# SyncE's queue in program order through the attention stage, pages fetched group by group, and gathers placed earlier in the program

## The chip, the cores and the metric

The kernel runs on one core of one Trainium2 chip. The metric is the device time of one execution in microseconds; of several executions the median is taken. Engines are named as in the profile: PE (matrix engine), DVE, ACT and POOL (vector, scalar and GpSimd engine), and SP, whose queue starts almost all transfers between HBM and on-chip memory. POOL starts the remaining ones, the gathers by a table of indices.

## What is computed

One layer of a decoder, for a prompt of 512 tokens and, with the same weights, for 8 samples that each have one new token and 1024 cached ones. D_MODEL is 1024, every tensor is f32. Two attention mixers read the same modulated input; "a" has three branches (compressed, selected, window), "b" (MoBA) picks blocks:

```python
h = x * (1.0 + scale[:, None, :]) + shift[:, None, :]
parts = jnp.split(h @ w_in, np.cumsum(IN_WIDTHS)[:-1], axis=-1)
(a_q, a_kc, a_vc, a_ks, a_vs, a_kw, a_vw, a_g, a_z, b_q, b_k, b_v, b_z, m_a, m_b) = parts
...
y_a = (o_a.reshape(bsz, t, NSA_WIDTH) * jax.nn.silu(a_z)) @ w_up_a
y_b = (o_b.reshape(bsz, t, MOBA_WIDTH) * jax.nn.silu(b_z)) @ w_up_b
mixed = (jax.nn.sigmoid(m_a) * y_a + jax.nn.sigmoid(m_b) * y_b) @ w_out
x_new = layer_norm(DEEPNORM_ALPHA * x + gate[:, None, :] * mixed, ln_g, ln_b)
```

For the samples the past rows of the caches come page by page: `rows = pool[page_table, layer]`. The layer also returns the new K and V rows.

## The kernel before

The whole layer is one program. Its parts, in the order of time:

- **Up to about 160 us**: the modulation, the compression network (`phi_*`) of the prompt and of the samples' cached rows (the stage `phis`), and the first projections.
- **About 160 to 520 us, the attention stage**: a loop over eight steps `pi`. Each runs `attend(pi)` (the prompt's attention of one or two heads at a time), a share of `dec()` (the samples' attention over their cached rows) and the projections listed in `FILLS[pi + 1]`. `merge` interleaves these three generators by the costs that their `yield`s name, so the numbers `ATT`, `DEC_SHARE` and `DEC` and the `yield`s decide in which order the program is written.
- **About 520 to 555 us**: `FILLS[9]`, that is the last projections (`bz2`, `bz3`, `m7`) and the gates `g0` to `g3`, merged with the rest of `dec()`.
- **To the end**: the matrices `w_up`, `w_out`, the normalisation and the output.

A **projection** (`dense`) is 48 matmuls of 260 columns into `d`: the 128 weight columns of one `w_cols` item, split into a high and a low half (`hl`; ACT makes the high part on L302, DVE or POOL the low part on L219), against the transposed input `hTh`, `hTl`. The items are loaded by the object `W`, a `Feed` over a ring of four buffers `raw`. `g0` to `g3` are items of `ada_g`, used unsplit by the matmuls `s<-raw,cs`. What a projection leaves goes on by name: `m0` to `m6` go through ACT as `mg` (L666) to HBM (`m_d`, L669) and are read back (`m_d` to `kd`, `v2`, `m`, L1376) when the attention's buffers are free; K and V rows are copied out as `ok<-ev` (L575); V rows are turned on PE and copied by DVE (`v`, L600, and `vnew`, L605). Work of that kind that need not follow at once is put on a list by `post`, and popped during the next projection.

The **samples' part** `dec()` reads 64 KB to 1 MB pieces of the caches into two buffers `raw` of 2048 columns, by the object `C`, also a `Feed`: `take` loads the next item when one is taken. The items, in order: four of `slck` (16 pages each), two of `wink`, 16 of `mobk` (4 pages each), then `slcv` gathers and `winv`, then 16 of `mobv` (4 pages each). Each item feeds one group of matmuls `e<-raw,...` on PE. `load_pages` reads a page's number from the page table into a register of SP (L728) and starts one transfer per page (L732). A `slcv` item is two gathers by POOL of 512 KB each (L1160). They stand behind the last POOL instruction `p` of the attention that was written so far (`issue_after(D["pool"].ins)`). `dec()` ends with `dec_b`: own scores and values of the new tokens (`snew`, `np`), then the `mobv` groups.

The **order of the queues**: a scheduler at build time orders the instructions of each engine by its own estimate of their times, except where the program fixes an order. Before, the program fixes PE's order through the attention stage (`behind`, L181 to L194) and leaves SP's order to the scheduler, with `tc.high_priority()` on the loads of `W` (`W.first`), on `ok<-ev` and on the writes to `m_d`. When the attention ends, `behind` is switched off; PE's further work is only kept behind the last attention instruction (`D["floor"]`). On POOL, `qx` (L996) makes the second operand for the scores of the next heads, and `p` (L1045) scales the probabilities of each score tile. `prepare(pi + 1)` issues `q`, `qx` and the `band` table (L983, L450) for the next step.

Of the kernel before, what the change touches and what calls it, by code (L numbers as in the profile page):

```python
# [46 lines left out]
DEC_SHARE = [0.155, 0.28, 0.405, 0.53, 0.59, 0.645, 0.74, 0.855]  # L47
DEC, DEC_PACE = 57600.0, 0.85
# [115 lines left out]
def build(tc, A):  # L164
# [3 lines left out]
    glue, behind = [False, None], [False, None]  # L168
# [12 lines left out]
    def in_turn(i):  # L181

        D["pe"] = i
        if "floor" in D:
            order(i, D["floor"])
# [38 lines left out]
    with ExitStack() as es:  # L224
# [35 lines left out]
        class Feed:  # L260


            def __init__(self, items, pool, tag, width, nraw, nhl=0):
                self.pool, self.tag, self.width, self.nraw, self.nhl = pool, tag, width, nraw, nhl
                self.loads = [(fn, n) for fn, n, _ in items]
                self.units = [(i, v) for i, (_, _, vs) in enumerate(items) for v in vs]
                self.raw, self.part = {}, {}
                self.nl = self.ns = 0
                self.used = -1
                self.apart = ()  # L270
                self.after = None
                self.first = False

            def load_to(self, i):
                while self.nl <= i and self.nl < len(self.loads):
                    fn, n = self.loads[self.nl]
                    t = self.pool.tile([128, self.width], F32, name="raw", tag=self.tag + "r", bufs=self.nraw)
                    if self.first:
                        with tc.high_priority():
                            fn(t[:, :n])  # L280
                    elif self.after is None:
# [41 lines left out]
        def w_item(n):  # L323
            if n == "ag":
                return (lambda t: nc.sync.dma_start(t, A["w_ag"])), 192, [lambda r: r[:, :192]]
# [8 lines left out]
            return (lambda t: nc.sync.dma_start(t, src)), 1024, HALVES  # L334
# [255 lines left out]
        def gen_v(name, vi):  # L590
            ev = evac((yield from dense(name)), name)

            def prompt():
# [6 lines left out]
                nc.vector.tensor_copy(v, p)  # L600

            def rest():
                p = p_d()
                tr(p[:NS, :128], ev[:, T:], ident)
                nc.vector.tensor_copy(vnew[:, vi, :], p[:NS, :128])  # L605
# [52 lines left out]
        def gen_m(c):  # L658
# [3 lines left out]
            for i, n in enumerate(("ma", "mb")):  # L662
# [4 lines left out]
                if "fm" not in D:  # L667
                    with tc.high_priority():
                        nc.sync.dma_start(m_d[c][:, i], to)  # L669
# [53 lines left out]
        def load_pages(outs, name, k0, step=1):  # L723
# [7 lines left out]
            for out, page in zip(outs, pages):  # L731
                dyn.append(nc.sync.dma_start(out, A[name][bass.ds(page, 1)].rearrange("a p c -> p (a c)")))  # L732
# [16 lines left out]
        def units(n, rhs):  # L749

            us = []
            for kv in range(2):
                u = p_s()
                for l in range(8):
                    for j, (wa, x) in enumerate(((w1h, 0), (w1l, 0), (w1h, 1))):
                        r = rhs(kv, x, l)
                        o = u[:, :n + 2] if n == 64 else u[:, :n]
                        mm(o, wa[:, kv, l, :], r, l == 0 and j == 0, l == 7 and j == 2)
# [29 lines left out]
        def phi_prompt(kc, vc):  # L788
            ut = []
            for kv, ev in enumerate((kc, vc)):  # L790
# [8 lines left out]
                for x, cp in enumerate((nc.scalar.copy, nc.vector.tensor_copy)):  # L799
                    v = f32(eh[:, x]).rearrange("p (u l s) -> p l u s", l=8, s=2)  # L800
                    for g in range(2):
                        for l2 in range(2):
                            cp(ut[kv][OWN[l2], x, :, g * 32:g * 32 + 32], v[OWN[g], :, :, l2])
            gl = yield from units(64, lambda kv, x, l: ut[kv][:, x, l, :])
# [167 lines left out]

        W.first = True
# [5 lines left out]
        def prepare(pi):  # L979
# [3 lines left out]
            nc.sync.dma_start(bt, A["band"][pi])  # L983
# [49 lines left out]
        def probs(j, i, n, s):  # L1033
# [11 lines left out]
            D["pool"] = nc.gpsimd.tensor_scalar(pr, pr, sm[:, 3:4], j.gate(i), op0=OP.mult, op1=OP.mult)  # L1045
# [64 lines left out]
        def step(j, extra=()):  # L1110
# [12 lines left out]
            for f, arg in extra:  # L1123
                slots[2].append(lambda f=f, arg=arg: f(arg))
# [6 lines left out]
        def attend(pi):  # L1131
            js = jobs_of(pi)
            if pi < 7:
                prepare(pi + 1)
            for k, j in enumerate(js):
                ex = []
                if pi < 4 and k == 0:
                    ex = [(cmp_score, pi)]
                if pi < 4 and k == 1:
                    ex = [(cmp_turn, pi)]  # L1140
# [6 lines left out]
        def page_item(name, firsts, width, step=1):  # L1147
            def fn(t):
                for i, k in enumerate(firsts):
                    load_pages([t[:, c * width:c * width + width] for c in range(4 * i, 4 * i + 4)], name, k, step)  # L1150
            return fn, 2048, [None]

        def plain_item(name, k):
            return (lambda t: nc.sync.dma_start(t, A[name][k])), 2048, [None]

        def slcv_item(i):
            def fn(t):
                with tc.issue_after(D["pool"].ins):
                  for k in range(2):
                    nc.gpsimd.indirect_dma_start(out=t[:, k * 1024:k * 1024 + 1024], out_offset=None, in_=A["slcv"],  # L1160
                                                 in_offset=bass.IndirectOffsetOnAxis(ap=vidx[:, 2 * i + k:2 * i + k + 1], axis=0))
            return fn, 2048, [None]

        C = Feed([page_item("slck", [(4 * q + b4) * 8 + hf * 4 for b4 in range(4)], 128)
                  for hf in range(2) for q in range(2)]
                 + [plain_item("wink", q) for q in range(2)]
                 + [page_item("mobk", [b * 8 + hf * 4], 512) for hf in range(2) for b in range(NS)]
                 + [i for q in range(2) for i in (slcv_item(2 * q), slcv_item(2 * q + 1), plain_item("winv", q))]
                 + [page_item("mobv", [4 * q * 8 + k], 512, 8) for q in range(2) for k in range(8)],
                 de, "c", 2048, CRAW)  # L1170
        C.apart = set(range(len(C.loads)))

# [15 lines left out]
        def new_p(d):  # L1188
# [5 lines left out]
            yield 300  # L1194
# [7 lines left out]
        def dec_a():  # L1202

            C.load_to(1)
            yield 2500
            xs = de.tile([128, 1026], F32, name="xs", tag="x")
            for hf in range(2):
                s = p_e()
                for q in range(2):
# [9 lines left out]
            nc.sync.dma_start(xw[:, :512], A["bw"])  # L1219
            less_last(xw[:, :512], xw[:, :512], brow[:, 0:1])  # L1220
            for q in range(2):
# [4 lines left out]
                if q == 0:  # L1226
                    yield 1000
# [3 lines left out]
            nc.vector.tensor_copy(xs[:, 1024:1025], snew[:, 0:1])  # L1231
# [8 lines left out]
            for g in range(2):  # L1240
                nc.vector.tensor_copy(view(zm[OWN[g]], g, [[NS * 32, 4], [34, NS]]), y[OWN[g], 4:8, T:])
# [6 lines left out]
            for hf in range(2):  # L1248
                s = p_e()
                for b in range(NS):  # L1250
# [6 lines left out]
                    yield 1000  # L1257
# [7 lines left out]
            for q in range(2):  # L1265
# [7 lines left out]
                yield 2700  # L1273
# [7 lines left out]
                yield 1400  # L1281

        def dec_b():
# [3 lines left out]
            nc.sync.dma_start(masks, A["cst"][:, NC2:NC3])  # L1287
# [7 lines left out]
            yield 300  # L1295
            total()
            yield 300
# [26 lines left out]
            for q in range(2):  # L1324
                o = p_e()
                for k in range(8):
# [4 lines left out]
                    yield 1000  # L1331
# [25 lines left out]
        for pi in range(8):  # L1357
# [7 lines left out]
            done = DEC_SHARE[pi]  # L1365
        at_es.close()
        behind[0] = False
        D["floor"] = D["pe"]
# [385 lines left out]
```

## Time and profile before

| | |
|---|---|
| median of 3 runs | 690.44 us (687.56 to 694.62) |
| the profiled execution, its own time | 692.0 us |
| its span in the trace | 690.2 us |
| mean clock granted to PE | 0.953 of full speed |
| DVE, ACT, POOL busy | 320.3, 297.0, 287.4 us |
| moved by DMA | 124.80 MB, 181 GB/s over the span |

A table of waits names, per engine and line, what an instruction stood waiting for. A table of windows gives for each stretch of time the busy time of each engine, the clock that PE was granted, and how busy the DMA engines were (1.00 is all 16 of them all the time). A line of the timeline starts with the start and the length of a piece of work in microseconds, then engine, line, operation and the tensors (out<-in); brackets at its end give the engine's idle time before it and what ended it. PE's matmuls overlap, so the length of one is longer than its share of a run of them. "SPq" and "POOLq" mean the issuing queue, and `x10` that ten like pieces stand in one line.

### The profile page before, as it was taken

The page shows a single profiled execution, that of the slowest core. Times are in us where ns is not written, and L with a number is a line of the kernel's source. Part 1 is how long each engine was busy: PE and PEld are TensorE (multiplying, and loading weights), DVE is VectorE, ACT ScalarE, POOL GpSimd, SP SyncE. Part 2 cuts the span into 40 slices and gives each one's busy share as a digit, 9 for nine tenths or more (in the row PEclk, how much of TensorE's full clock was granted, in tenths as well). Part 3 has the DMA queues.
Part 4 walks back from the last instruction along what each step waited for, and adds up shares of the span by engine and source line. Part 5 has one row for each costly group of instructions (what it writes and reads, how often), then busy time and mean ns, then how long its engine had stood idle before and what let it go on. Part 6 is the DMA issues. An engine that isn't in the chain of part 4 may idle for free.

```text
span 690.2 us, 13240 instructions
## 1 busy us (share of the span) xinstructions
PE 613.8 (89%) x4709; PEld 514.0 (74%) x4709; DVE 320.3 (46%) x817; ACT 297.0 (43%) x678; POOL 287.4 (42%) x327
## 2 busy tenths in 40 slices
PE   5999799999766999999993939989998879999993
PEld 3788799999754788777763838986775568899673
DVE  3464455525732744544641414665430115655167
ACT  3365455534442654544550525554441124333422
POOL 2033747523532434334542624534420126566546
PEclk9999999999997999999996979999999799999997
DMA  8984566413555627767743445423978873244303
GB/s 316 398 290 140 142 179 196 126 62 105 183 164 165 231 95 239 238 206 249 227 136 115 142 137 204 148 99 96 313 255 295 312 290 120 73 156 152 113 1 124
DMA packets 63956, 124.80 MB, mean 181 GB/s; under 512 B 8402, under 2 KB 26642, under 8 KB 63378
## 3 DMA queue, kind: packets, MB, share of 16 engines
q1 hardware_dynamic: 62482, 119.76, 52.5%
q0 software_dynamic: 1408, 4.20, 2.0%
q8 instruction: 37, 0.61, 0.4%
q14 instruction: 29, 0.24, 0.1%
HBM read 114.34 MB, written 9.58 MB: 180 GB/s over the span
## 4 chain that ended last, share of the span: by engine, by line
PE 69%; DMA 9%; DVE 6%; issue 5%; SPq 4%; POOL 4%; ACT 3%; POOLq 0%; DVEq 0%; ACTq 0%
PE d L172 39%; PE s L172 11%; PE e L172 6%; PE pt L193 3%; SPq L732 3%; PE o L172 3%; PE o L175 3%; DMA raw<-slcv,vidx 2%; DMA raw<-mobv 2%; PE pt L172 2%; PE e L175 1%; DMA u<-ada_ss 1%; POOL hl L219 1%; DMA m_d<-mg 1%; DMA craw<-cmp 1%
## 5 line engine op out<-in xcount | busy, mean ns | idle before, releaser
L172 PE MATMUL d<-hTh,hl 128*128 128x260 f32 (+1 forms) x1408 | 282.0, 296 | 4.6 <-ACT hl L302 2.8
L172 PEld LDWEIGHTS d<-hTh,hl 128*128 128x128 f32 (+1 forms) x1408 | 223.3, 192 | 33.4 <-issue 22.8
L172 PE MATMUL d<-hTl,hl 128*128 128x260 f32 (+1 forms) x704 | 202.2, 288 | 0.0
L172 PEld LDWEIGHTS d<-hTl,hl 128*128 128x128 f32 (+1 forms) x704 | 134.8, 191 | 1.1 <-issue 0.8
L219 POOL TENSOR_TENSOR hl<-raw,hl 128x512 fp32r<-128x512 f32 x54 | 70.9, 1313 | 74.2 <-ACT hl L302 60.7
L302 ACT CAST hl<-raw 128x512 fp32r<-128x512 f32 (+1 forms) x111 | 68.0, 617 | 77.7 <-PE d L172 57.9
L1043 ACT ACTIVATE p<-s,sm 128x512 f32<-128x512 f32 (+1 forms) x96 | 50.7, 529 | 93.9 <-DVE sm L1040 88.1
L1045 POOL TENSOR_SCALAR p<-p,sm,gp 128x512 f32<-128x512 f32 (+1 forms) x64 | 41.1, 642 | 108.0 <-DVE sm L1044 105.8
L219 DVE TENSOR_TENSOR hl<-raw,hl 128x512 fp32r<-128x512 f32 (+1 forms) x57 | 53.3, 936 | 48.3 <-ACT hl L302 47.3
L172 PE MATMUL d<-yh,hl 128*128 128x260 f32 x256 | 46.8, 284 | 1.8 <-DVE ev L1421 1.8
L1040 DVE CUSTOM_DVE_ANT_0 s<-s,band 128x256 f32<-128x256 f32 (+1 forms) x48 | 17.5, 364 | 64.8 <-PE s L172 62.8
L172 PE MATMUL e<-raw,tp 128*32 128x512 f32 (+1 forms) x40 | 20.5, 598 | 25.6 <-DMA raw<-slcv,vidx 21.3
L172 PEld LDWEIGHTS d<-yh,hl 128*128 128x128 f32 x256 | 39.6, 188 | 3.3 <-DVE ev L1421 2.2
L1038 DVE TENSOR_REDUCE sm<-s 128x1 f32<-128x256 f32 (+1 forms) x48 | 17.0, 355 | 52.4 <-PE s L172 50.9
L193 PE MATMUL pt<-cst,p 128*128 128x128 f32 x240 | 39.7, 281 | 0.7 <-DVE pp L1054 0.7
L1045 POOL TENSOR_SCALAR p<-p,sm,cst 128x512 f32<-128x512 f32 (+3 forms) x32 | 20.5, 641 | 41.6 <-DVE sm L1044 34.9
L172 PE MATMUL d<-yl,hl 128*128 128x260 f32 x128 | 35.9, 284 | 0.0
L172 PE MATMUL s<-u,w1h 128*128 128x256 f32 (+1 forms) x160 | 30.7, 287 | 4.3 <-ACT u L839 2.7
L219 POOL TENSOR_TENSOR u<-craw,u 128x512 fp32r<-128x512 f32 x16 | 22.1, 1389 | 29.5 <-ACT u L839 29.5
L193 PEld LDWEIGHTS pt<-cst,p 128*128 128x128 f32 x240 | 29.0, 144 | 6.5 <-DVE sm L1044 2.5
L172 PE MATMUL s<-kd,q 128*128 128x512 f32 (+1 forms) x96 | 32.8, 342 | 0.0
L1054 ACT COPY pp<-pt 128x512 f32<-128x512 f32 (+1 forms) x48 | 23.0, 480 | 19.9 <-PE pt L193 19.7
(414 smaller groups left out, 1168.0 us busy)
## 6 DMA issues: line engine op xcount, KB each, us to landing
raw<-w_cols SPq DMA_DIRECT2D x46, 512.0 KB, 3.9
raw<-mobk SPq DMA_DIRECT2D x64, 256.0 KB, 4.1
raw<-mobv SPq DMA_DIRECT2D x64, 256.0 KB, 4.2
craw<-cmp SPq DMA_DIRECT2D x64, 128.0 KB, 2.3
u<-ada_ss SPq DMA_DIRECT2D x12, 512.0 KB, 9.0
raw<-slck SPq DMA_DIRECT2D x64, 64.0 KB, 2.1
raw<-ada_g SPq DMA_DIRECT2D x8, 512.0 KB, 5.1
raw<-w_up SPq DMA_DIRECT2D x8, 512.0 KB, 5.2
```

Of the source, the lines that this page charges most:

```text
L172: i = mmraw(out, lhsT, rhs, start=start, stop=stop, skip_group_check=True)
L175: i = mmraw(out, lhsT, rhs, start=start, stop=stop, skip_group_check=True)
L193: return in_turn(nc.tensor.transpose(out, x, unit))
L219: (nc.gpsimd if eng == "p" else nc.vector).tensor_sub(out, x, f32(hi))
L302: nc.scalar.copy(h, src)
L732: dyn.append(nc.sync.dma_start(out, A[name][bass.ds(page, 1)].rearrange("a p c -> p (a c)")))
L1038: nc.vector.tensor_reduce(sm[:, 0:1], s[:, :b], axis=AX, op=OP.min)
L1040: nc.vector.tensor_tensor_reduce(out=s[:, b:n], in0=s[:, b:n], in1=j.band[:, 256 - (n - b):], scale=1.0, scalar=top, op0=OP.add, op1=OP.mi ...
L1043: nc.scalar.activation(pr, s[:, :n], AF.Exp, scale=-1.0, bias=sm[:, 1:2], accum_out=sm[:, 2:3])
L1045: D["pool"] = nc.gpsimd.tensor_scalar(pr, pr, sm[:, 3:4], j.gate(i), op0=OP.mult, op1=OP.mult)
L1054: j.copied[gi] = (nc.scalar.copy if COPY_ENG[gi] == "a" else nc.vector.tensor_copy)(t[:, :n], p[:, :n])
```

## The change

- **SP's queue.** A new helper `ld` starts every transfer of SP; between the opening of the attention's pools and the end of `FILLS[9]` each is chained behind the one before it in the program (`queue`). The high priorities of the loads go. `ok<-ev` and the writes to `m_d` are put on the `post` list, so they stand in the program during the next projection.
- **Pages.** `Feed` for the caches is replaced by `Pages`: the next item is fetched behind the group that frees its buffer, page quad by page quad, with a `yield` after each quad.
- **Gathers.** They stand behind the last but one `p` instead of the last, and by `Pages` they come behind the group that frees their buffer.
- **PE's order** stays fixed until the end of `FILLS[9]`; the `floor` goes. The posts are emptied at the attention's end, and the reads of `m_d` stand there in SP's order.
- **Smaller moves.** `prepare(pi + 1)` goes from ahead of a step to the end of its first job; copies of V rows get a high priority on DVE; the `zm` copies come later; the first matmul of a compression unit is ordered; shares and `yield`s change.

```diff
-DEC_SHARE = [0.155, 0.28, 0.405, 0.53, 0.59, 0.645, 0.74, 0.855]
-DEC, DEC_PACE = 57600.0, 0.85
+DEC_SHARE = [0.1, 0.236, 0.375, 0.51, 0.575, 0.63, 0.765, 0.89]
+DEC, DEC_PACE = 58800.0, 0.9
...
+    def ld(out, x):
+
+        i = nc.sync.dma_start(out, x)
+        if queue[0]:
+            if queue[1] is not None:
+                order(i, queue[1])
+            queue[1] = i
+        return i
...
-            with tc.high_priority() if W.first else ExitStack():
-                nc.sync.dma_start(A["ok"][KOUT.index(name)], ev)
+            post(lambda: ld(A["ok"][KOUT.index(name)], ev))
...
-                nc.vector.tensor_copy(v, p)
+                with tc.high_priority() if behind[0] else ExitStack():
+                    nc.vector.tensor_copy(v, p)
...
-                    with tc.high_priority():
-                        nc.sync.dma_start(m_d[c][:, i], to)
+                    post(lambda to=to, i=i: ld(m_d[c][:, i], to))
...
-            if pi < 7:
-                prepare(pi + 1)
             for k, j in enumerate(js):
-                ex = []
+                ex = [(3, prepare, pi + 1)] if pi < 7 and k == 0 else []
...
-                with tc.issue_after(D["pool"].ins):
...
+                with tc.issue_after(D["pool"][-2].ins):
...
+        class Pages:
+            def __init__(self, items):
+                self.items, self.tiles = iter(items), []
+            def fetch(self, cost=0):
+                item = next(self.items, ())
+                if item:
+                    t = de.tile([128, 2048], F32, name="raw", tag="cr", bufs=CRAW)
+                for fn in item:
+                    fn(t)
+                    yield cost / len(item)
+                if item:
+                    self.tiles.append(t)
+                else:
+                    yield cost
+            def take(self):
+                return self.tiles.pop(0)
...
-            C.load_to(1)
-            yield 2500
+            drain(C.fetch())
+            yield from C.fetch(2600)
...
-                    yield 1500
+                    yield from C.fetch(1200 if hf and q else 2000)
...
-                    yield 1000
+                    yield from C.fetch(1600 if hf and b == NS - 1 else 850)
...
-                yield 2700
+                yield from C.fetch()
+                yield from C.fetch(2300)
...
-                    yield 1000
+                    yield from C.fetch(1000)
...
+        while posts:
+            posts.pop(0)()
         at_es.close()
-        behind[0] = False
-        D["floor"] = D["pe"]
...
-            nc.sync.dma_start(TM[c], m_d[c])
+            ld(TM[c], m_d[c])
         merge(Flow(fills(FILLS[9]), fill_cost(FILLS[9])), Flow(part(2.0), max(1.0, (1 - done) * DEC / DEC_PACE)))
-        D.pop("floor")
-        assert not posts
+        while posts:
+            posts.pop(0)()
+        behind[0] = queue[0] = False
```

Two places show how instructions move. The first is POOL's queue around the first two pairs of `slcv` gathers (`raw<-slcv`, two of 512 KB in each row). In the kernel before, the second pair, `raw_4851`, stands behind `qx_4405` and the `p` that follows it:

```order
L1160 DMA raw_4755<-slcv,vidx_77 128x1024 x2
L1045 TENSOR_SCALAR p_4769<-p_4769,sm_4766,gp_80 128x384
L1045 TENSOR_SCALAR p_4791<-p_4791,sm_4789,gp_80 128x256
L996 TENSOR_TENSOR qx_4405<-y_95,q2_4404 64x512
L1045 TENSOR_SCALAR p_4830<-p_4830,sm_4828,gp_80 128x128
L1160 DMA raw_4851<-slcv,vidx_77 128x1024 x2
L1045 TENSOR_SCALAR p_4894<-p_4894,sm_4891,gp_80 128x512
```

In the changed kernel the same stretch of POOL's queue reads:

```order
L1163 DMA raw_4749<-slcv,vidx_77 128x1024 x2
L1051 TENSOR_SCALAR p_4732<-p_4732,sm_4729,gp_80 128x512
L1051 TENSOR_SCALAR p_4764<-p_4764,sm_4761,gp_80 128x384
L1163 DMA raw_4801<-slcv,vidx_77 128x1024 x2
L1051 TENSOR_SCALAR p_4786<-p_4786,sm_4784,gp_80 128x256
L1002 TENSOR_TENSOR qx_4561<-y_95,q2_4560 64x512
L1051 TENSOR_SCALAR p_4832<-p_4832,sm_4830,gp_80 128x128
```

The second pair has moved from behind `qx` to ahead of it, three instructions earlier, and the first pair stands one `p` earlier.

The second place is SP's queue at the attention's end, where the last write to `m_d`, its seven reads, the gates' `ada_g` and the weights of `bz3` (`raw<-w_cols`) stand among the `mobv` pages. In the kernel before, with the pages and register loads between them left out, the queue reads:

```order
L1376 DMA v2_6608<-m_d_94 128x1040
L334 DMA raw_6475<-ada_g 128x1024
...
L334 DMA raw_6738<-ada_g 128x1024
L1376 DMA v2_6610<-m_d_94 128x1040
L669 DMA m_d_94<-mg_6592 128x520
...
L1376 DMA m_6612<-m_d_94 128x1040
L1376 DMA m_6614<-m_d_94 128x1040
...
L334 DMA raw_6740<-w_cols 128x1024
L334 DMA raw_6746<-ada_g 128x1024
```

In the changed kernel, from the last write to `m_d` on, again without the pages (two `mobv` items stand between `raw_6671` and `raw_6768`):

```order
L199 DMA m_d_94<-mg_6645 128x520
L199 DMA kd_6655<-m_d_94 128x1040
L199 DMA kd_6657<-m_d_94 128x1040
L199 DMA kd_6659<-m_d_94 128x1040
L199 DMA v2_6661<-m_d_94 128x1040
L199 DMA v2_6663<-m_d_94 128x1040
L199 DMA m_6665<-m_d_94 128x1040
L199 DMA m_6667<-m_d_94 128x1040
L199 DMA raw_6671<-ada_g 128x1024
...
L199 DMA raw_6768<-ada_g 128x1024
L199 DMA raw_6770<-ada_g 128x1024
L199 DMA raw_6772<-w_cols 128x1024
```

All seven reads now stand together behind the last write, and three of the first four `ada_g` loads behind the reads; before, four `ada_g` loads and five reads stood ahead of that write.

More of the change, by code (lines that the diff above doesn't have):

```diff
@@ L166, in build @@
     mmraw = nc.tensor.matmul
-    glue, behind = [False, None], [False, None]
+    glue, behind, queue = [False, None], [False, None], [False, None]
     def mm(out, lhsT, rhs, start, stop):
@@ L604, in rest @@
                 tr(p[:NS, :128], ev[:, T:], ident)
-                nc.vector.tensor_copy(vnew[:, vi, :], p[:NS, :128])
+                with tc.high_priority() if behind[0] else ExitStack():
+                    nc.vector.tensor_copy(vnew[:, vi, :], p[:NS, :128])
             post(prompt)
@@ L731, in load_pages @@
             for out, page in zip(outs, pages):
-                dyn.append(nc.sync.dma_start(out, A[name][bass.ds(page, 1)].rearrange("a p c -> p (a c)")))
+                dyn.append(ld(out, A[name][bass.ds(page, 1)].rearrange("a p c -> p (a c)")))
         def phi_start():
@@ L757, in units @@
                         o = u[:, :n + 2] if n == 64 else u[:, :n]
-                        mm(o, wa[:, kv, l, :], r, l == 0 and j == 0, l == 7 and j == 2)
+                        before = D["pe"]
+                        i = mm(o, wa[:, kv, l, :], r, l == 0 and j == 0, l == 7 and j == 2)
+                        if kv == l == j == 0:
+                            order(i, before)
                     yield 333
@@ L971, in build @@
         at = D["at"] = open_pool(at_es, "at", "right")
-        W.first = True
+        queue[0] = True
         pc = at.tile([128, T], F32, name="pc")
@@ L1147, in page_item @@
         def page_item(name, firsts, width, step=1):
[L1148 to L1151, printed above, removed]
+            return [lambda t, i=i, k=k: load_pages([t[:, c * width:c * width + width] for c in range(4 * i, 4 * i + 4)], name, k, step)
+                    for i, k in enumerate(firsts)]
         def plain_item(name, k):
-            return (lambda t: nc.sync.dma_start(t, A[name][k])), 2048, [None]
+            return [lambda t: ld(t, A[name][k])]
@@ L1156, in slcv_item @@
         def slcv_item(i):
             def fn(t):
-                with tc.issue_after(D["pool"].ins):
[L1159 to L1170, printed above, removed]
@@ L1171, in build @@
-        C.apart = set(range(len(C.loads)))
+                with tc.issue_after(D["pool"][-2].ins):
+                    for k in range(2):
+                        nc.gpsimd.indirect_dma_start(out=t[:, k * 1024:k * 1024 + 1024], out_offset=None, in_=A["slcv"],
+                                                     in_offset=bass.IndirectOffsetOnAxis(ap=vidx[:, 2 * i + k:2 * i + k + 1], axis=0))
+            return [fn]
+        class Pages:
[14 more added lines that the diff above has]
+                return self.tiles.pop(0)
@@ new lines, in build @@
+        C = Pages([page_item("slck", [(4 * q + b4) * 8 + hf * 4 for b4 in range(4)], 128)
+                   for hf in range(2) for q in range(2)]
+                  + [plain_item("wink", q) for q in range(2)]
+                  + [page_item("mobk", [b * 8 + hf * 4], 512) for hf in range(2) for b in range(NS)]
+                  + [i for q in range(2) for i in (slcv_item(2 * q), slcv_item(2 * q + 1), plain_item("winv", q))]
+                  + [page_item("mobv", [4 * q * 8 + k], 512, 8) for q in range(2) for k in range(8)])
@@ L1230, in dec_a @@
             nc.vector.tensor_add(xs[:, 896:1024], xs[:, 896:1024], bdn[:, 0:128])
-            nc.vector.tensor_copy(xs[:, 1024:1025], snew[:, 0:1])
+            late = nc.vector.tensor_copy(xs[:, 1024:1025], snew[:, 0:1])
             xv = xs[:, 64:960].rearrange("p (j c) -> p j c", j=14)
@@ L1240, in dec_a @@
             for g in range(2):
-                nc.vector.tensor_copy(view(zm[OWN[g]], g, [[NS * 32, 4], [34, NS]]), y[OWN[g], 4:8, T:])
+                with tc.issue_after(late.ins):
+                    nc.vector.tensor_copy(view(zm[OWN[g]], g, [[NS * 32, 4], [34, NS]]), y[OWN[g], 4:8, T:])
             yield 1500
@@ L1280, in dec_a @@
                 nc.scalar.copy(xo[:, q], on[:, :128])
-                yield 1400
+                yield from C.fetch(1800)
         def dec_b():
```

38 lines of the change are left out of this document (16 added, 22 removed).

## The prediction

> **What bounds the kernel now.** I read the busy times first, then PE's waits, then windows by stage, then the timeline around each long wait.
>
> ```profile
> span 690.2 us, 13240 instructions
> PE 613.8 (89%) x4709; PEld 514.0 (74%) x4709; DVE 320.3 (46%) x817; ACT 297.0 (43%) x678; POOL 287.4 (42%) x327
> ...
> PE e L172 <- DMA raw<-slcv,vidx: 21.3, 2, 10.9
> PE e L172 <- DMA raw<-slck: 11.1, 3, 5.2
> PE e L172 <- DMA raw<-mobv: 4.3, 3, 2.3
> PE d L193 <- DVE v L600: 3.5, 1, 3.5
> PE s L172 <- ACT u L839: 2.7, 1, 2.7
> PE e L172 <- DVE snew L899: 1.6, 1, 1.6
> PE e L172 <- DVE np L1193: 1.5, 1, 1.5
> ...
> 230.00:285.00 55.00, 55.00 (x427) 43.90 (x426) 27.08 (x95) 31.25 (x81) 21.21 (x25) 1.00 0.57 184
> 528.00:540.00 12.00, 7.98 (x57) 3.70 (x55) 0.85 (x2) 2.50 (x5) 1.88 (x3) 0.84 1.00 369
> ```
>
> PE is the bound: 613.8 of 690.2 us, and in 230 to 285 it is busy all the time at full clock. The change adds no matmul worth counting, so what it can win is PE's idle time and the slow clock behind it. The waits that it touches are the samples' pages (`slck`, `slcv`, `mobv`) and small chains. In windows the columns are length, then busy time of PE, PEld, DVE, ACT and POOL, the granted clock, the DMA share and GB/s. At 528 to 540 the DMA engines are the limit: share 1.00 at 369 GB/s.
>
> A wait costs more than its length where the clock falls behind it:
>
> ```profile
> 208.88 1.03 PE L172 MATMUL e<-raw,zn 128*32 128x512 f32 x1 [5.20 <-DMA raw<-slck]
> 220.78 1.03 PE L172 MATMUL e<-raw,zn 128*32 128x512 f32 x1 [4.66 <-DMA raw<-slck]
> 373.47 0.39 PE L172 MATMUL e<-raw,tp 128*32 128x128 f32 x1 [10.89 <-DMA raw<-slcv,vidx]
> 408.40 0.42 PE L172 MATMUL e<-raw,tp 128*32 128x128 f32 x1 [10.38 <-DMA raw<-slcv,vidx]
> ...
> 208.80:212.80 4.00, 3.92 (x20) 2.28 (x21) 0.49 (x2) 0.40 (x2) 0.00 (x0) 0.60 0.41 116
> 220.70:226.20 5.50, 5.42 (x24) 3.64 (x25) 2.30 (x4) 1.21 (x2) 0.87 (x1) 0.55 0.85 320
> 373.40:379.40 6.00, 5.93 (x73) 5.38 (x74) 0.98 (x3) 0.00 (x0) 0.00 (x0) 0.51 0.20 51
> 408.30:414.30 6.00, 5.90 (x78) 5.29 (x79) 0.00 (x0) 0.37 (x1) 0.00 (x0) 0.58 0.18 40
> 537.50:546.90 9.40, 8.76 (x39) 6.73 (x40) 1.34 (x1) 1.14 (x2) 1.27 (x1) 0.52 1.04 397
> 459.80:479.80 20.00, 18.18 (x119) 14.36 (x121) 12.74 (x36) 8.64 (x24) 8.76 (x10) 0.83 0.12 33
> ```
>
> Busy time times one minus the clock is what the slow clock cost: 3.92 x 0.40 = 1.6 and 5.42 x 0.45 = 2.4 after the `slck` waits, 5.93 x 0.49 = 2.9 and 5.90 x 0.42 = 2.5 after the `slcv` waits. With its tail, `slck` costs 11.1 + 4.0 = 15.1 us, the first `slcv` pair 10.89 + 2.9 = 13.8, the second 10.38 + 2.5 = 12.9.
>
> **The change, part by part.** `slck`, first. The price of a page group is SP's issue time and the landing:
>
> ```profile
> 192.18 10.51 SPq L732 DMA_DIRECT2D raw<-slck  x15
> raw<-mobv SPq DMA_DIRECT2D x64, 256.0 KB, 4.2
> ...
> raw<-slck SPq DMA_DIRECT2D x64, 64.0 KB, 2.1
> 516.91 1.43 PE d L172 x12
> ```
>
> 15 issues in 10.51 us are 0.70 each, so a group of 16 needs 11.2 + 2.1 = 13.3 us from the group that frees its buffer. In the instruction order of before, 48 projection matmuls stand between that group's end and the use (48 x 0.12 from the 1.43 us row is 5.7 us, and 9.7 to 11.2 with the scores, turns and values among them). Behind the change it is 96, and 72 for the last, 16.4 to 19.4 us in all. That is above 13.3 by 3 to 6 us, even with a weight load or an `m_d` write between the pages. The first two groups are fetched from the stage's start as before, and SP's queue works them off in a row. I leave 1 us of the 15.1: gain 14 (ends 7, if pages queue behind waits for ACT, and 15).
>
> The first `slcv` pair. POOL's timeline before:
>
> ```profile
> 357.06 1.06 POOL L1160 DMA_INDIRECT raw<-slcv,vidx  x1 [0.30 <-issue]
> 358.43 0.96 POOL L1160 DMA_INDIRECT raw<-slcv,vidx  x1 [0.30 <-issue]
> 365.28 1.26 POOL L996 TENSOR_TENSOR qx<-y,q 64x512 fp32r<-64x512 f32 x1 [2.19 <-DMA raw<-slcv,vidx]
> 366.64 0.45 POOL L1045 TENSOR_SCALAR p<-p,sm,gp 128x128 f32<-128x128 f32 x1
> 367.41 1.04 POOL L1160 DMA_INDIRECT raw<-slcv,vidx  x1 [0.31 <-issue]
> 368.75 0.95 POOL L1160 DMA_INDIRECT raw<-slcv,vidx  x1 [0.30 <-issue]
> ...
> 355.51 0.61 PE L175 MATMUL e<-raw,zm 128*32 128x512 f32 x3
> ```
>
> The second half was issued at 367.41 only because `qx` ahead of it stood until the first half had landed (365.28), though its buffer was free when the last `mobk` group ended at 356.1. It landed at 373.47, 4.7 us behind its second issue; the first half took 6.7 (358.43 to about 365.1). Behind the change the second half is ahead of `qx`: issue at about 357.4 and 358.7, landed at 363.4 to 365.4. But `qx` now waits for both halves, and `p_4832` behind it for `qx` (1.26 + 0.45): 365.1 to 367.1. PE needs that `p` in a turn that stands about 4.4 us of work behind the `mobk` group (361.0 at the least with the small gaps of before), so PE stands there 4 to 6 us, and no longer at the gather. I take 5 us with the clock's part: gain 13.8 - 5 = 8.8. Ends: 3 us left (gain 11) and 11 left (gain 3, rival C).
>
> A stall of 4 to 6 us lies where the traces say two things of the clock:
>
> ```profile
> 175.26 3.08 DVE L450 TENSOR_SCALAR band<-band,tab 128x256 f32<-128x256 f32 x4
> 179.59 0.27 PE L193 MATMUL d<-cst,ev 128*8 128x128 f32 x1 [3.51 <-DVE v L600]
> 179.62 0.48 PE L172 MATMUL d<-hTh,hl 128*128 128x260 f32 x2
> ```
>
> After 3.51 us of idleness the matmuls run at full speed (0.48 for two of 260 columns; behind the 10.38 us wait such a pair took 0.80); after 4.66 the clock was 0.55. [...]
>
> The second pair is issued, in the order of POOL, ahead of the scores' `p`s that delayed it, some 7 to 8 us of PE work before its use, with about 4.7 us to land. I leave 1 us: gain 12 (ends 7 and 13). The V copy (L600) stood behind four `band` pieces of 3.08 us; high priority and `prepare` moved to a job's end take about half of 3.5: gain 1.5 (0 to 3). Gains together: 14 + 8.8 + 12 + 1.5 = 36.3.
>
> Now what it loses. At `dec_b`'s head (459.80 to 479.80) the waits `snew` and `np` are 1.6 + 1.5, and the clock took 18.18 x 0.17 = 3.1. Its chain has 4.8 us of other PE work in its longest link where it had 6.3, so about 1.5 more idle and as much clock: loss 3 (0 to 5). The `mobk` and `mobv` groups need 4 page issues at 0.6 and a landing of 4.2 us, 6.6 us in all, between use and reuse; the order gives 5.4 to 10.2: loss 1 (0 to 4). The fills between the compression units, where PE waited 2.7 us on `u` of L839 once, give 10.1 to 10.4 us of cover for 11.3 to 12.7: loss 2 (0 to 4).
>
> The tail is the largest loss. The chain of waits and the transfers there:
>
> ```profile
> 522.95 4.57 DMA m_d<-mg
> ...
> 531.41 6.06 DMA raw<-mobv
> ...
> 534.84 0.62 PE L172 MATMUL e<-raw,tp 128*32 128x512 f32 x1 [2.34 <-DMA raw<-mobv]
> 537.52 1.06 PE L172 MATMUL e<-raw,tp 128*32 128x512 f32 x1 [1.61 <-DMA raw<-mobv]
> 540.87 0.59 PE L172 MATMUL d<-hTh,hl 128*128 128x260 f32 x1 [0.55 <-POOL hl L219]
> ```
>
> Before, PE stood 2.34 + 1.61 + 0.55 = 4.5 us here and lost 8.76 x 0.48 = 4.2 to the clock: 8.7. Four `ada_g` and five of the seven `m_d` reads had gone by then. Behind the change, SP issues between the last `m_d` write and the first gates: that write (0.27 MB), seven reads (3.7 MB), three `ada_g` (1.6) and two `mobv` items (2.1), 7.65 MB, all before the weights of `bz3`. At the 369 GB/s of 528 to 540 that is 20.7 us, and the weights' split (ACT and POOL, about 2 us) follows: `bz3` starts some 23.5 us behind the write. PE has about 10.6 us of work until there, so it stands 13, and with the same 4.2 of clock the place costs 17; I take 19, since the last read also waits the 4.57 us for the write's landing and SP's later pages stand behind it. The loss is 19 - 8.7 = 10.3, and 1.7 more for the gates and `ada_g` that follow in a row: 12. Ends: 2, if the reads spread out, and 22, if no transfer overlaps that landing and a second slow stretch follows.
>
> [...]
>
> The sum: -36.3 + 3 + 1 + 2 + 12 = -18.3. The span would go from 690.2 to 671.9, the profiled execution from its 692.0 us (1.8 around the span) to 673.7. That execution lies 1.6 above the median of 690.44; from the median it is 672.1. I say 672.
>
> **The rivals.**
> A: the tail is hidden. The seven reads fall into PE's 10 us of work, `ada_g` lands in time, and the tail loses 2 instead of 12: 662. For it: with the DMA engines full, PE stood there only 4.5 us before. Against it: DMA share 1.00 at 528 to 540 already before.
> B, slower: SP's fixed queue blocks at its head. A transfer of the weights waits until POOL or DVE has freed its ring buffer, and all pages behind it wait with it, at each of the 32 `mobk` and `mobv` groups. It loses 32 us for each microsecond that a group comes late beyond its room; with 0.6 the gain of 18.3 is gone, with 0.8 it is past 697, and 1 us gives 704. For it: the room is 5.4 to 10.2 us against 6.6 needed. Against it: at 230 to 285 PE is never idle with the same two buffers and the same rings.
> C: the wait of the first pair only moves. `qx` waits for a slow second half (6.7 us and contention of the two halves), PE stands 11 us at the turn: gain 3, time 678; with the second pair likewise at 7, 683.
> D: the queue does not bring the pages earlier. 64 `slck` pages at 0.70 are 45 us of SP, and with writes waiting for ACT between them the waits stay: gain 0 instead of 14, time 686.
>
> **How the numbers follow.** Forecast 0.55, A 0.17, C 0.10, D 0.08, B 0.10. The forecast's terms reach from 664 (tail 6, first pair 11) to 682 (tail 18, `slck` 10). The range takes in A and C and D, from 659 to 687, and leaves out most of B and a little of the rest. One per cent, about what a measurement of this kernel can tell from no change, puts the bounds at 683.5 and 697.3. Faster: 0.53 of the forecast, A's 0.17 and 0.06 of C, 0.76. Within 1%: 0.02 of the forecast, 0.04 of C, D's 0.08 and 0.03 of B, 0.17. Slower: the rest of B, 0.07.
>
> **What would show it.** Right: no PE wait on `raw<-slck` above 2 us; the second half of the gather issued a few us behind the first; a PE wait of 4 to 6 us on POOL's `p` or on the pages' landing near the first `slcv` group, and at most 2 us at the second; windows at 230 to 340 still full; behind the last `m_d` write a stretch with DMA share near 1.00 and a PE wait of 10 us or more before `bz3`. Wrong: waits on `mobk` or `mobv` in many groups (B), `slck` waits of 4 us and more (D), or a tail with under 6 us of idleness (A).

## The result and the profile after

The changed kernel takes 667.23 us (median of 4 runs, 664.64 to 671.92) against 691.33 us (4 runs) of the kernel before, a ratio of 0.9661 with the 95% interval 0.9586 to 0.9735. The prediction was 672, 659 to 687. The profiled execution took 666.75 us with a span of 665.0, so the span is 25.2 us shorter. First the page's head, then PE's waits (us in total, times, longest):

```profile
span 665.0 us, 13243 instructions
PE 605.9 (91%) x4709; PEld 504.1 (76%) x4709; DVE 320.0 (48%) x817; ACT 296.0 (45%) x678; POOL 288.2 (43%) x327
...
PE s L172 <- DMA raw<-ada_g: 18.6, 3, 6.6
...
PE pt L191 <- POOL p L1051: 5.1, 1, 5.1
PE pt L191 <- ACT pp L1060: 3.2, 2, 2.5
...
PE e L172 <- DMA raw<-winv: 2.4, 1, 2.4
PE d L172 <- DVE v L603: 1.7, 1, 1.7
...
PE e L172 <- DVE snew L906: 0.9, 1, 0.9
PE e L191 <- DVE sm L1050: 0.9, 1, 0.9
...
PE e L172 <- DVE xn L1344: 0.8, 1, 0.8
```

The rows for `slck` (11.1) and `slcv` (21.3) are gone and `mobv` is down from 4.3 to 0.2. In their place stand three waits on `ada_g`, one on POOL's `p`, one on `winv`, and one on ACT's `pp` that has grown from 0.8 to 2.5 us. The timeline of PE places them:

```profile
193.87 1.06 PE L191 MATMUL pt<-cst,c 128*64 128x128 f32 x4 [2.52 <-ACT pp L1060]
355.37 1.12 PE L191 MATMUL pt<-cst,p 128*128 128x128 f32 x4 [5.13 <-POOL p L1051]
371.89 0.30 PE L172 MATMUL e<-raw,tp 128*32 128x128 f32 x1 [2.42 <-DMA raw<-winv]
506.26 1.06 PE L172 MATMUL s<-raw,cs 128*32 128x512 f32 x1 [5.75 <-DMA raw<-ada_g]
514.51 1.06 PE L172 MATMUL s<-raw,cs 128*32 128x512 f32 x1 [6.32 <-DMA raw<-ada_g]
532.49 1.06 PE L172 MATMUL s<-raw,cs 128*32 128x512 f32 x1 [6.55 <-DMA raw<-ada_g]
```

The windows show what the slow clock added behind them, and that it is gone at 431 to 445 (length, busy PE, PEld, DVE, ACT, POOL, clock, DMA share, GB/s):

```profile
193.80:199.80 6.00, 5.93 (x27) 4.04 (x28) 1.14 (x5) 1.05 (x4) 0.97 (x2) 0.51 0.53 158
355.30:361.30 6.00, 5.93 (x22) 3.85 (x24) 1.11 (x4) 0.00 (x0) 2.66 (x4) 0.50 0.00 0
431.00:445.00 14.00, 11.64 (x93) 9.41 (x94) 10.60 (x33) 7.96 (x22) 7.41 (x9) 1.00 0.05 19
500.00:514.50 14.50, 2.44 (x13) 0.50 (x11) 0.42 (x1) 0.39 (x1) 1.41 (x2) 0.62 1.03 406
514.50:532.50 18.00, 11.43 (x82) 6.85 (x82) 2.20 (x3) 2.40 (x5) 2.69 (x3) 0.88 0.75 272
532.50:545.00 12.50, 12.50 (x83) 8.54 (x83) 2.72 (x3) 4.04 (x8) 2.73 (x3) 0.79 0.57 199
```

Behind the first two waits PE loses 5.93 x 0.49 = 2.9 and 5.93 x 0.50 = 3.0 us. At `dec_b`'s head (431 to 445) the clock is full, where it was 0.83. At the tail it takes 2.44 x 0.38 + 11.43 x 0.12 + 12.5 x 0.21 = 4.9 us, so the tail costs 18.6 + 4.9 = 23.5 us.

The last write to `m_d` divides the program. SP's timeline after, and before (start, length):

```profile
492.81 0.33 SPq L199 DMA_DIRECT2D m_d<-mg  x1
493.20 1.40 SPq L199 DMA_DIRECT2D kd<-m_d  x3
494.64 0.94 SPq L199 DMA_DIRECT2D v<-m_d  x2
495.68 0.98 SPq L199 DMA_DIRECT2D m<-m_d  x2
496.71 0.70 SPq L199 DMA_DIRECT2D raw<-ada_g  x1
498.58 7.99 SPq L199 DMA_DIRECT2D raw<-mobv  x8
506.91 1.08 SPq L199 DMA_DIRECT2D raw<-ada_g  x2
```

```profile
522.95 0.33 SPq L669 DMA_DIRECT2D m_d<-mg  x1
```

Until that write, 522.95 - 492.81 = 30.1 us are won. From there to the first matmul against `yh` it was 50.0 us (572.97) and is 58.7 (551.54), so 8.7 are given back, and the rest of the program is 3.8 us shorter.

### The profile page after: what moved, and what is told of

Read it like the earlier page. It is cut to its first block, busy times and chain, and to the rows that moved or that the text cites. A ratio compares the mean times of both kernels' runs of the same rounds, so it can differ in the third digit from the quotient of the medians.

```text
span 665.0 us, 13243 instructions
## 1 busy us (share of the span) xinstructions
PE 605.9 (91%) x4709; PEld 504.1 (76%) x4709; DVE 320.0 (48%) x817; ACT 296.0 (45%) x678; POOL 288.2 (43%) x327
## 4 chain that ended last, share of the span: by engine, by line
PE 66%; DMA 14%; DVE 5%; ACT 4%; SPq 4%; issue 4%; POOL 2%; POOLq 0%; ACTq 0%; DVEq 0%
PE d L172 37%; PE s L172 9%; PE e L172 7%; PE pt L191 4%; DMA raw<-w_cols 4%; SPq L199 3%; PE o L175 3%; PE o L172 3%; DMA craw<-cmp 2%; DMA raw<-mobv 2%; DMA raw<-ada_g 2%; DMA y<-ada_ss 1%; DMA xr<-xT 1%; PE pt L172 1%; PE e L175 1%
## 5 line engine op out<-in xcount | busy, mean ns | idle before, releaser
L172 PE MATMUL d<-hTh,hl 128*128 128x260 f32 (+1 forms) x1408 | 277.9, 293 | 1.7 <-DVE v L603 1.7
L172 PEld LDWEIGHTS d<-hTh,hl 128*128 128x128 f32 (+1 forms) x1408 | 219.5, 189 | 26.7 <-issue 18.1
L172 PEld LDWEIGHTS d<-hTl,hl 128*128 128x128 f32 (+1 forms) x704 | 132.6, 188 | 0.5
L226 POOL TENSOR_TENSOR hl<-raw,hl 128x512 fp32r<-128x512 f32 x55 | 72.7, 1322 | 64.1 <-ACT hl L305 43.2
L1046 DVE CUSTOM_DVE_ANT_0 s<-s,band 128x256 f32<-128x256 f32 (+1 forms) x48 | 17.4, 363 | 48.7 <-PE s L172 45.8
L191 PEld LDWEIGHTS pt<-cst,p 128*128 128x128 f32 x240 | 27.6, 142 | 16.7 <-POOL p L1051 8.0
L172 PE MATMUL s<-kd,qx 128*128 128x512 f32 (+1 forms) x96 | 31.0, 323 | 0.0
L175 PE MATMUL o<-pp,v 128*64 128x384 f32 (+3 forms) x168 | 30.6, 437 | 0.0
L1002 POOL TENSOR_TENSOR qx<-y,q 64x512 fp32r<-64x512 f32 x16 | 24.2, 1512 | 14.6 <-ACT q L999 9.5
```

The costliest lines, as they stand in the source:

```text
L172: i = mmraw(out, lhsT, rhs, start=start, stop=stop, skip_group_check=True)
L175: i = mmraw(out, lhsT, rhs, start=start, stop=stop, skip_group_check=True)
L191: return in_turn(nc.tensor.transpose(out, x, unit))
L226: (nc.gpsimd if eng == "p" else nc.vector).tensor_sub(out, x, f32(hi))
L1002: nc.gpsimd.tensor_sub(qx[own], y[own, pi, :T], f32(q2[own]))
L1046: nc.vector.tensor_tensor_reduce(out=s[:, b:n], in0=s[:, b:n], in1=j.band[:, 256 - (n - b):], scale=1.0, scalar=top, op0=OP.add, op1=OP.mi ...
```

## The experiments

Each is the changed kernel with the edit shown, timed beside the kernel before on the same chip; the ratio is to that one. The median counts every execution, the profiled one too, which the ratio leaves out. A profile is of one execution, which can lie at the edge of the range.

**Late reads.** The loop over the seven reads goes behind the merge:

```diff
-        for c in range(D.get("put", 0)):
-            TM[c] = m_tile(F32, TM_TAGS[c])
-            ld(TM[c], m_d[c])
         merge(Flow(fills(FILLS[9]), ...), ...)
+        for c in range(D.get("put", 0)):
+            TM[c] = m_tile(F32, TM_TAGS[c])
+            ld(TM[c], m_d[c])
```

> The changed kernel, with the seven reads of m_d moved behind the merge of FILLS[9] in the program, so behind the gates' ada_g loads in SP's queue. Theory (the reads' burst makes the gates wait): the first two waits on ada_g, 5.75 + 6.32 us, fall to at most 3 us together, the third (6.55) stays; 8 to 12 us less than the changed kernel, 655 to 660. Rival (the bytes only move, and w_up or the first use of the read-back tiles waits instead): under 3 us less, with a new PE wait behind 550 us.

Measured: 660.60 us (659.77 to 660.91), ratio 0.9554 (0.9536 to 0.9572). PE's timeline has two waits on `ada_g` left:

```profile
509.48 1.06 PE L172 MATMUL s<-raw,cs 128*32 128x512 f32 x1 [6.88 <-DMA raw<-ada_g]
526.96 1.06 PE L172 MATMUL s<-raw,cs 128*32 128x512 f32 x1 [5.08 <-DMA raw<-ada_g]
```

The reads' burst cost 6.6 us of time, less than the 8 to 12 expected: the first gate no longer waits, but the second still does. Its `ada_g` pair was issued at 502.11, behind eight `mobv` pages, half a microsecond before PE was ready for it. No wait came behind 550 us.

**One gate item ahead.**

```diff
                     mm(p[grp(k)], cs[...], raw[...], kp == 0, kp == 1)
+            W.load_to(W.units[W.used][0] + NRAW)
             yield 1000
```

> The changed kernel, with one line that loads the next weight item straight behind a gate's matmuls, so that one more ada_g item stands ahead of the mobv pages in SP's queue. Theory (ada_g stands behind pages that wait for PE): the third wait of 6.55 us on ada_g shrinks by half or more, 3 to 9 us less than the changed kernel (658 to 664). Rival (bandwidth is the limit there, so the load lands no earlier): within 2 us of the changed kernel, the wait stays above 5 us.

Measured: 666.58 us, ratio 0.9636 (0.9615 to 0.9658); the third wait is 4.85 us where it was 6.55. Only one of the pair could go ahead, since `bz3`'s weights hold the ring's other buffer, and a gate needs both. It tells nothing against the order as the cause, and it did not win the 3 to 9 us expected.

**The second qx on DVE.**

```diff
-                nc.gpsimd.tensor_sub(qx[own], y[own, pi, :T], f32(q2[own]))
+                (nc.vector if g else nc.gpsimd).tensor_sub(qx[own], y[own, pi, :T], f32(q2[own]))
```

> The changed kernel, with the second qx of each prepare on DVE instead of POOL. Theory (the 5.13 us wait on POOL's p is only qx standing on POOL until the gathers have landed): the wait is gone, and the 3.0 us of slow clock behind it; the slcv group waits at most 1 us; 6 to 9 us less than the changed kernel (658 to 661). Rival 1 (the wait moves to the gather's landing at the slcv group): 3 us less or under. Rival 2 (DVE's eight more operations delay the score chains): no gain or slower.

Measured: 664.26 us (656.58 to 669.90), ratio 0.9638 (0.9592 to 0.9685). In PE's timeline the turn waits 0.72 us instead of 5.13, and the `slcv` group does not wait:

```profile
348.66 0.65 PE L191 MATMUL pt<-cst,p 128*128 128x128 f32 x4 [0.72 <-POOL p L1051]
354.05 0.30 PE L172 MATMUL e<-raw,tp 128*32 128x128 f32 x1
361.24 0.30 PE L172 MATMUL e<-raw,tp 128*32 128x128 f32 x1 [2.29 <-DMA raw<-winv]
```

The mechanism is shown: POOL's `qx` was what held PE. Why a `qx`, which reads nothing of the gather, waits for its landing is not shown; the `qx` behind the second pair's first half did not (at 369.19 in the changed kernel, right behind the issue at 368.22). The time of this run alone does not show the gain, since its executions lie 13 us apart and the profile is of the fastest, 656.58 us; the run with late reads and `qx` on DVE below does.

**Weights out of the chain.**

```diff
-            return (lambda t: ld(t, src)), 1024, HALVES
+            def fn(t):
+                with tc.high_priority() if queue[0] else ExitStack():
+                    nc.sync.dma_start(t, src)
+            return fn, 1024, HALVES
```

> The changed kernel, with the loads of the weight ring taken out of SP's chain and given high priority again, while pages, writes and reads stay chained. Theory (the 2.52 us wait at 193.9 comes from a weight load behind slck pages, whose split then blocks ACT's queue): that wait is under 1 us and its 2.9 us of slow clock is gone, 4 to 6 us less, and the gates' ada_g come earlier too, so 4 to 15 us less than the changed kernel. Rival (the chain of all transfers is what keeps the pages on time): waits on slck, mobk or mobv come back, 5 us slower or more.

Measured: 667.76 us, ratio 0.9685 (0.9642 to 0.9728). In SP's timeline the weight load that came at 188.40 now comes at 187.67 with one more ahead of it at 180.48, and `pp` waits are at most 1.5 us. But the tail has other waits instead:

```profile
PE e L172 <- DMA raw<-mobv: 8.0, 2, 6.2
PE d L172 <- ACT hl L305: 7.3, 2, 5.0
```

So the early wait does come from the weight load's place (it is 0.81 us here). The 4 to 15 us expected did not come: the tail's new waits stand against what was gained.

**The chain off.** The line `queue[0] = True` is left out.

> The changed kernel, with SP's chain off: the scheduler places the transfers, while the fetches behind the group, the gathers' place, the shares and PE's fixed order stay. Theory (the waits on pages and gathers went because fetches and PE work were spaced apart, and the chain by itself only costs at the tail and at the weight load near 194 us): no slck wait above 2 us, the three ada_g waits of 18.6 us are halved, 5 to 15 us less than the changed kernel (652 to 662). Rival (the chain brings the pages on time): waits on slck of 4 us and more are back, 675 us or more.

Measured: 668.85 us (659.96 to 673.15), ratio 0.9694 (0.9642 to 0.9745). There is no `slck`, `slcv` or `ada_g` wait in its profile, which is of the fastest execution. The turn's wait on `p` stays, and the tail's waits are on the weights' split and on `mobv`:

```profile
PE d L172 <- ACT hl L305: 8.5, 2, 4.9
...
PE pt L191 <- POOL p L1050: 6.0, 1, 6.0
...
PE e L172 <- DMA raw<-mobv: 2.9, 4, 2.0
```

The chain by itself neither won nor lost time that these runs could tell. So the gain of the change is in the other parts. The runs below try two of them, the gathers' place and the shares; the place of the fetch, PE's order to the end and the smaller moves have no run of their own. That the chain costs 5 to 15 us, as I had expected, is not borne out.

**Gathers behind the last p.**

```diff
-                with tc.issue_after(D["pool"][-2].ins):
+                with tc.issue_after(D["pool"][-1].ins):
```

> The changed kernel, with the gathers behind the last p instead of the last but one. Theory (the early place behind the group that frees the buffer does most of it; qx waits for both halves in either place): POOL issues the second half one p later, so the wait on POOL's p grows by 1 to 2 us, and the time is within 3 us of the changed kernel. Rival (the place behind the last but one p is what took the second half ahead of qx): the 10 us waits on slcv are back, 10 to 20 us slower than the changed kernel.

Measured: 670.53 us, ratio 0.9688 (0.9654 to 0.9722), 3.3 above the median of the changed kernel; the wait on `p` is 7.2 us instead of 5.1. The 10 us waits do not return, so it is not the step back by one `p` that took the second half ahead of `qx`. The fetch behind the freeing group did it, or the later place of `prepare`, which issues `qx`; no run parts the two. The step back by one `p` is worth about 2 us by the wait; the times alone do not tell the runs apart.

**The shares of before.** `DEC_SHARE`, `DEC` and `DEC_PACE` get their old numbers.

> The changed kernel, with the numbers DEC_SHARE, DEC and DEC_PACE of before. Theory (what took away the slck waits is twice the PE work between a group and the one after next, which these numbers and the yields set): with larger shares in the first steps that work shrinks to 11 to 15 us against 13.3 needed, and 2 to 10 us of slck waits come back; 2 to 10 us slower than the changed kernel. Rival (the order of SP alone does it): no slck wait, within 2 us of the changed kernel.

Measured: 681.03 us (677.09 to 686.68), ratio 0.9830 (0.9784 to 0.9876), by medians 13.8 us above the changed kernel and by ratios 11.7. PE's waits again have pages in them:

```profile
PE s L172 <- DMA raw<-ada_g: 14.8, 2, 7.5
PE e L172 <- DMA raw<-mobv: 10.2, 1, 10.2
...
PE e L172 <- DMA raw<-slck: 5.9, 3, 4.4
```

Between a `slck` group and the one after next its program has 66 projection matmuls instead of 96. By its own trace that is 14.6 us of PE work from the first group's end (196.90) to the third (217.41, less 5.9 us of waits), more than the 13.3 us that a group needs from the release of its buffer, and 4.44 us of wait came all the same. SP's timeline tells why:

```profile
182.91 13.05 SPq L199 DMA_DIRECT2D raw<-slck  x20
...
205.20 1.89 SPq L199 DMA_DIRECT2D raw<-slck  x4
```

The first page of the third group, the 33rd, was issued at 205.20, 8.3 us after its buffer was free: until then SP was at the second group's pages. SP took 43.1 us for all 64 pages and what stands between them (182.91 to 225.99), 10.8 us a group, and PE had only 8.8 and 7.1 us of work from one of the first three groups to the next. The chain was on, and the waits came back, so PE's spacing counts, but against SP's rate. The 10.2 us at `mobv` was not expected, and is more of the loss than `slck`.

**The tail in another order.** Late reads, the line of the second experiment, and the ring's loads one item further ahead in the last stage:

```diff
-                self.load_to(self.units[u][0] + 2)
+                self.load_to(self.units[u][0] + (3 + (u > 0 and self.units[u - 1][0] == self.units[u][0]) if "fm" in D else 2))
```

> The changed kernel, with the m_d reads behind the merge as in the run with late reads, and the ring's loads one item further ahead in the last stage, so that each pair of ada_g items stands ahead of the mobv pages that wait for PE. Theory (what is left of the tail's wait is ada_g behind pages that wait for PE's groups): the waits on ada_g fall from 12.0 us with late reads alone to under 5, and 3 to 9 us less than that run: 651 to 658. Rival (bandwidth): the wait moves to mobv or the weights of bz3 and the time stays within 2 us of 660.6.

Measured: 662.70 us (656.78 to 665.74), ratio 0.9555 (0.9501 to 0.9609), no better than late reads alone. The waits on `ada_g` shrink to one of 1.67 us, and the weights of `bz3` and `ma7` are late instead:

```profile
505.53 0.62 PE L172 MATMUL s<-raw,cs 128*32 128x512 f32 x1 [1.67 <-DMA raw<-ada_g]
510.28 0.39 PE L172 MATMUL d<-hTh,hl 128*128 128x260 f32 x1 [2.83 <-ACT hl L305]
527.58 0.58 PE L172 MATMUL d<-hTh,hl 128*128 128x260 f32 x1 [4.64 <-ACT hl L305]
```

The rival held: without the reads, what goes first only chooses which load is waited for. Whether bandwidth alone sets that is open; the DMA share from 485 to 545 was 0.80 there, not 1.00.

**Late reads and qx on DVE together.** The line of the second experiment is in it too, which the expectation does not say.

> The changed kernel, with late m_d reads and the second qx on DVE together. Theory (the two stalls are apart in time and add): the wait on POOL's p under 1 us and the ada_g waits near 12 us; 10 to 14 us less than the changed kernel, 653 to 657, and 3 to 7 less than late reads alone (660.6). Rival (with the median of the qx run only 3 us lower, the wait's place is refilled): within 2 us of 660.6.

Measured: 654.13 us (651.97 to 656.94, 6 runs), ratio 0.9457 (0.9423 to 0.9492). It is 12.5 us under the changed kernel run beside it, and the fastest of all. Late reads alone gave 6.6 us by medians and `qx` alone 3.0, so neither takes the other's gain away. Against late reads alone it wins another 6.7 us by ratios, and the intervals lie apart. The added line had won nothing alone, and the waits on `ada_g` are 11.6 us here and 12.0 with late reads alone, so `qx` is the likely cause of that gain:

```profile
span 653.4 us, 13256 instructions
...
PE s L172 <- DMA raw<-ada_g: 11.6, 2, 7.1
PE pt L191 <- ACT pp L1061: 6.9, 4, 3.2
...
PE pt L191 <- POOL p L1052: 0.7, 1, 0.7
```

**The yields of dec_b's head.** The yields of 500, 700 and 600 there become 300 again, as before.

> The changed kernel, with the three yields near the head of dec_b as before (300 each instead of 500, 700 and 600). Theory (the head's waits shrank from 3.4 us and 3.1 us of slow clock because these numbers put more other PE work between its links): the waits on snew, sm, tp and xn of 2.9 us grow to 4 to 7 us, and the time by 2 to 7 us. Rival (the smaller share of the samples before, so the finish of their first half comes while more is left, did it): waits stay within 1 us, time within 2 us.

Measured: 676.19 us (669.46 to 680.53), ratio 0.9724 (0.9666 to 0.9782). By medians that is 9.5 us more than the changed kernel beside it, by ratios, which leave out the execution of 680.53 us, 6.2, with intervals that just meet. Most of it is not where I looked: the waits at the head are 0.9, 1.7 and 0.8, hardly more than the 2.9 us of the changed kernel. In 433.5 to 447.5 PE is busy 11.32 of 14.00 us at a clock of 0.88, which is 1.4 us of slow clock where the changed kernel had none. More waiting is where the `mobv` groups follow closer (three waits, 3.5 us) and at `hl` in the tail (3.5). So these numbers probably matter, and the theory of where they act fell.

**Weights free until the attention ends**, on top of late reads and qx on DVE: the loads leave the chain only while `"fm" not in D`. The line of the second experiment is not in this run.

> Late reads and the second qx on DVE together, and the weight ring's loads out of the chain with high priority until the attention ends, chained again behind it. Theory (the wait at the compressed turn near 194 us is the weight load behind slck pages, and taking it out costs only in the tail): the wait on ACT's pp there is under 1.2 us, no slck wait above 2 us, and 2 to 5 us less than the run without this part. Rival (the free loads push pages late): waits on slck, mobk or mobv of 3 us and more, and no gain.

Measured: 661.12 us (655.69 to 665.61, 6 runs), ratio 0.9564 (0.9522 to 0.9606), 7 us more than the run above, from which it differs in two things. In its profile the wait near 194 us is 0.81 us as expected (at 189.88) and no `slck` wait appears, but `pp` has another wait of 4.1 us and `ada_g` 15.0 instead of 11.6. That profile is of its fastest execution, 655.69 us against 655.19 in the run above, so it does not show where the 7 us go. No step forward.

**The changed kernel again.**

> The changed kernel itself, again, beside the others of this group. Expected: 664 to 671 us, with the ada_g waits of 18 to 19 us, the wait on POOL's p of 4 to 7 us and the pp wait of 2 to 3 us in place; it gives the size against which the other runs of this group are read.

Measured: 666.65 us (665.00 to 671.08, 5 runs), ratio 0.9634 (0.9599 to 0.9668), with waits of 17.0 us on `ada_g`, 4.5 on POOL's `p` and 2.34 on `pp` at the same places, and two more on `pp`, of 1.43 and 2.06 us, later on.

## Why the prediction came out as it did

The sum said 18.3 us; the spans differ by 25.2. Term by term, from the two profiles:

- **slck, gain 14.** The waits and their slow clock, 15.1 us, are gone, and the run with the shares of before shows that PE's spacing is a reason. But the condition that I had priced, 13.3 us from the release of a buffer, is not what bound the kernel before. There the 33rd page was issued at 196.0, 5.7 us after its buffer was free (190.28): SP took 46.8 us for the 64 pages (171.64 to 218.43), 11.7 a group, and PE had 5.7 to 7.2 us of work from one group to the next. In the changed kernel SP took 45.8 us, hardly less, and PE asked every 10.2 to 12.2 us, the first time 21 us after the first page. And a wait of 2.52 us with 2.9 of slow clock has come where 0.81 was: a weight load issued at 188.40, behind twenty `slck` pages, on which ACT's `hl` (at 192.26, idle 2.14 before) and behind it `pp` stand. Net 10.5. That is the fixed queue of rival B the other way round, weights behind pages; I had not priced it.
- **First slcv pair, gain 8.8.** As described: the second half is issued at 345.83, `qx` waits for both halves until 353.50, PE waits at the turn for 5.13 us. The wait was sized rightly (4 to 6); the slow clock behind it was not: 3.0 us came on top, so the gain is 13.8 - 8.1 = 5.7. Of the two things that the traces had said of the clock, 0.55 behind 4.66 us was nearer here than full speed behind 3.51: it was 0.50 behind the 5.13 us.
- **Second pair, gain 12.** No wait on the gather; 2.42 us on `winv` behind it: 10.5.
- **V copy, gain 1.5.** 3.51 to 1.70: 1.8.
- **dec_b's head, loss 3.** This step failed in its sign. The waits went from 3.4 to 2.9 us, and 3.1 us of slow clock to none, a gain of 3.6. I had derived a longer idle link from less PE work in it. With the yields of before, 0.5 us of waits and 1.4 of slow clock came back in the one profile, so the new yields are not most of it; what is stays open.
- **mobk and mobv, loss 1, and the compression units, loss 2.** No wait above 0.2 us, and about 0.6.
- **The tail, loss 12.** 23.5 us now. Before it was 8.7, and 2.82 + 0.84 us of waits on the split near 556 with 1.5 of slow clock belonged to the same stretch, 13.9 in all: loss 9.6. The cause was right, as late reads show, with 6.6 us from the reads alone. The place was not: I had PE stand once, before `bz3`; it stood at three gates. In part that is SP's order, in which the pairs of `ada_g` wait behind pages; putting them ahead only moved the wait.

These add up to 10.5 + 5.7 + 10.5 + 1.8 + 3.6 - 0.6 - 9.6 = 21.9, and 1.8 more are the waits on `ev` behind 573, which are gone. The remaining 1.5 us I can't place. Part of the nearness is luck: the gains were forecast 7.8 us too large (36.3, measured 28.5) and the losses 11.4 too large (18, measured 6.6), and the two errors cancel for the most part. The slow stretch in the `slck` term is not in every execution either, as the last section shows.

Rival A did not happen, since the tail lost, and neither did D; C happened in part, with 8.1 of its 11 us. What the title names first, the queue in program order, made no difference that the run with the chain off could tell; the sum had priced spacing and place.

## What to carry to other kernels

Where a double-buffered stream of small loads makes the matrix engine wait, compare the time that the queue takes to issue a group with the matrix engine's work from one group to the next, before touching the order of the queue: here 10.8 to 11.7 us a group stood against 5.7 to 7.2 before and 10.2 to 12.2 after, and a chain on the queue made no difference that could be told. When a transfer is moved earlier, look at which instruction of the issuing engine then waits for its landing and who stands behind it: here POOL stood idle for 4.23 us ahead of `qx`, until 353.50, and PE 5.13 us behind it. Reads that nobody needs yet belong behind the loads that are waited for (late reads took 6.6 us less here), and two stalls that are apart in time can be taken out one by one: the run with both edits was 12.5 us faster.

## What the runs showed of the hardware

How long PE idles did not fix whether its clock falls. The same turn near 194 us is followed by slow matmuls in the changed kernel's first profile. In its second, and after an even longer wait in the run with late reads and `qx` on DVE, the clock is full for the next 6 us (the turn, then the window behind it, for each):

```profile
198.34 0.63 PE L191 MATMUL pt<-cst,c 128*64 128x128 f32 x4 [2.34 <-ACT pp L1060]
198.30:204.30 6.00, 5.96 (x46) 4.97 (x47) 2.02 (x8) 2.55 (x7) 2.24 (x3) 1.00 0.49 133
```

```profile
194.72 0.63 PE L191 MATMUL pt<-cst,c 128*64 128x128 f32 x4 [3.21 <-ACT pp L1061]
194.70:200.70 6.00, 5.99 (x46) 4.99 (x47) 2.02 (x8) 2.57 (x7) 2.22 (x3) 1.00 0.48 121
```

The first profile has 1.06 us after 2.52 us of idleness and a clock of 0.51, against 0.63 us and a clock of 1.00 in the other two. A stretch as slow as the first (5.93 us busy at 0.51) is worth some 3 us, and executions of one kernel here lie up to 13 us apart, with granted clocks of 0.953 to 0.977 in those with `qx` on DVE alone. So a single execution can't tell an edit worth 3 us, and a slow stretch seen in one profile is not yet a property of the kernel.
